# A decoder step on one core: the opening of the kernel, where the input is turned and split

## The chip, the cores and the metric

The kernel runs on one core of one Trainium2 chip. The metric is the time of one execution in microseconds (us) of device time; several executions are made and the median is taken. The profile of one execution gives, for each engine of the core, when each instruction ran: TensorE (PE, matrix products, with its weight loads shown apart as PEld), VectorE (DVE), ScalarE (ACT), GpSimd (POOL) and SyncE (SP, which here only issues transfers). An engine's letters with a q behind them (ACTq, SPq) are its queue, which issues transfers and waits.

## The reference

A two-layer decoder makes one step for a prompt of 512 tokens and for 8 samples of one token each, all in float32 and with the same weights. Layer 0 mixes tokens by causal pooling, layer 1 by sliding-window attention with sinks. Both layers have a SwiGLU block before and after the mixer. Only the first block matters for what follows:

```python
D_MODEL = 1024
D_FF = 2816

def _rmsnorm(x, g):
    xf = x.astype(jnp.float32)
    y = xf * lax.rsqrt(jnp.mean(xf * xf, axis=-1, keepdims=True) + EPS)
    return (y * g.astype(jnp.float32)).astype(x.dtype)

def _swiglu(x, wg, wu, wd):
    return (jax.nn.silu(x @ wg) * (x @ wu)) @ wd

x = x + 0.5 * _swiglu(_rmsnorm(x, norm_g[l, 0]), ffn_w_gate[l, 0], ffn_w_up[l, 0], ffn_w_down[l, 0])
```

## The kernel before, in words

**Layout.** Tokens lie along the free side: 512 prompt tokens and 8 samples make 520 columns, and the 1024 features make 8 tiles of 128 partitions, `x[0]` to `x[7]`. Each float32 operand of a product is split into a high part and a low part, and a product is made of three terms: high by high, low by high, high by low. ScalarE makes the high part (a copy that rounds), VectorE the low part (the rest). For the input the names are `xh` and `xl`, for a piece of 128x512 weights `wh` (line 194) and `wl` (line 195). The 520 columns are taken as two halves of 260, so one feature tile against one weight piece is six products of 260 columns (line 417).

**The opening (lines 657 to 736).** The input arrives as rows, so it must be turned. `load_x(eng, c, b2)` loads a block `xt` of two token tiles by 256 features; there are 4 columns `c` by 2 halves `b2`, and each block serves two feature tiles. `xs` are the samples' rows, `grow` the rows of the norms' gains, `grow2` three more rows of gains needed later. `W.begin(2)` issues the first two weight pieces, half of the gate and half of the up weights of the first output tile.

Then come twelve products of a tile of ones with itself (line 698), whose result nobody reads, the turn of the gains (line 699) and their copy `gT` (line 700). `x_tile(k)` turns one feature tile: four transposes (line 707) and one for the samples (line 709) into a pair of PSUM banks, `px`. Then ScalarE writes `xh` from the bank, scaled by the gain (line 712), the bank is copied to `x[k]` (odd k: ScalarE, line 714; even k: VectorE, line 716), and VectorE writes `xl` from `x[k]` (line 717).

The loop over the eight tiles makes the first tile of the gate and up outputs together, two accumulators called `first`. In round k it makes the six products of the gate output, turns tile k+2, and makes the six products of the up output. Its first weight pieces are fetched with `W.get()`, which splits a piece into `wh` and `wl`, ahead of the loop.

**What sets the order.** A scheduler orders each engine's instructions by a model of their times; everything wrapped in `later(...)` keeps its place in the program's order on its engine. Engines run their own list strictly in order and wait on semaphores. Transfers are issued by the SP, ACT and POOL lists in their order; every eighth transfer of SP and ACT together waits for the landing of the one eight before it. PSUM has four pairs of banks (`duo()`): one goes to the ones and the gains, two to `first`, the others turn over between feature tiles. A pair is free again once all its readers are done. In the built programs, before and after the change, the accumulator of the up output lies in the pair that tile 0 was turned in.

**What follows the loop.** The squares of each `x[k]` are summed for the norm (line 366 on ScalarE, lines 368 and 370 on VectorE), the next output tile runs `plain_tile`, and so on through the blocks.

Of the kernel before, what the change touches and what calls it, by code (L numbers as in the profile page):

```python
# [11 lines left out]
F32 = mybir.dt.float32  # L12
# [3 lines left out]
ALU = mybir.AluOpType  # L16
AX = mybir.AxisListType

P = 128
D = 1024  # L20
KT = 8
# [191 lines left out]
def yoco_step(ctx, tc, ins, outs):  # L213
    nc = tc.nc
# [3 lines left out]
    V, S, T = nc.vector, nc.scalar, nc.tensor  # L218
# [8 lines left out]
    def duo():  # L227

        cnt[0] += 1
        return psp.tile([P, 2, 512], F32, tag="ps", name=f"ps{cnt[0]}")  # L230
# [4 lines left out]
    def pair(tags, shape, dtype=F32R):  # L235

        return tuple(big.tile(shape, dtype, tag=t, name=t) for t in tags)
# [13 lines left out]
    def later(ins):  # L251

        return tc.keep_in_program_order(ins)
# [52 lines left out]
    for t in range(0, 8, 2):  # L306
        gp, i = t // 4, t % 4
# [39 lines left out]
    x = [cp.tile([P, TOK], F32, name=f"x{k}") for k in range(KT)]  # L347
    gT = cp.tile([P, 72], F32, name="gT")

    def gcol(n, k):  # L350
        return gT[:, n * 8 + k : n * 8 + k + 1]
# [12 lines left out]
    def square(k, pool, tag, order=lambda ins: ins):  # L364
        sq = pool.tile([P, TOK], F32, tag=tag, name="sq", bufs=1 if tag == "rp0" else 2)
        S.activation(sq, x[k], AF.Square)
        if k == 0:
            order(V.tensor_copy(acc[:, :TOK], sq))
        else:
            order(V.tensor_tensor(acc[:, :TOK], acc[:, :TOK], sq, op=ALU.add))  # L370
# [42 lines left out]
    def mm(w, kk, mov, banks, first, last, halves=(0, 1), pin=lambda ins: ins):  # L413

        for i, (a, b) in enumerate(terms(w, mov)):
            for hf in halves:
                ins = T.matmul(  # L417
                    banks[:, hf, :H],
                    a[:, kk, :],
                    hcols(b, hf),  # L420
                    start=(first and i == 0),
                    stop=(last and i == 2),
                )
                pin(ins)
# [202 lines left out]
    def ff_pool():  # L627
        return tc.tile_pool(name="ff", bufs=2)
# [31 lines left out]
    with ff_pool() as tmp:  # L660

        xv = x_prompt[0].rearrange("(b p) c -> p b c", p=P)
        xt = {}

        def load_x(eng, c, b2):
            xt[c, b2] = big.tile([P, 2, 256], F32, tag=TT[b2], name="xt")
            later(eng.dma_start(xt[c, b2], xv[:, 2 * b2 : 2 * b2 + 2, c * 256 : (c + 1) * 256]))

        grow = tmp.tile([48, P], F32, tag="g", name="grow")
        grow2 = tmp.tile([24, P], F32, tag="g", name="grow2")  # L670
        later(nc.scalar.dma_start(grow, norm_g.rearrange("l n (k p) -> (l n k) p", p=P)))
        xs = [big.tile([NS, 512], F32, tag=t, name="xs") for t in HH]
        for i in range(2):
            later(nc.scalar.dma_start(xs[i], x_sample[:, 0, i * 512 : (i + 1) * 512]))
        for b2 in range(2):
            load_x(nc.sync, 0, b2)
        W.begin(2)
        warm = cp.tile([P, 1], F32, name="warm")
        later(S.activation(warm, ones[:, 0:1], AF.Square))
        for b2 in range(2):  # L680
            load_x(nc.scalar, 1, b2)
        for b2 in range(2):
            load_x(nc.sync, 2, b2)
        W.load(0)
        for b2 in range(2):
            load_x(nc.sync, 3, b2)
        W.load(2)
        nc.gpsimd.dma_start(grow2[0:8, :], kv_norm_g.rearrange("(k p) -> k p", p=P))
        nc.gpsimd.dma_start(grow2[8:16, :], final_norm_g.rearrange("(k p) -> k p", p=P))
        nc.gpsimd.dma_start(grow2[16:24, :], pool_scale.rearrange("l (k p) -> (l k) p", p=P))  # L690
        sinks = cp.tile([P, 64], F32, name="sinks")
        nsinks = cp.tile([P, 64], F32, name="nsinks")
        sink_s = cp.tile([P, 2], F32, name="sink_s")
        sraw = cp.tile([P, 16], F32, name="sraw")
        mov0, tt = [], {}
        pd = duo()
        for i in range(12):
            later(T.matmul(pd[:, 1, :P], ones, ones, start=True, stop=True))  # L698
        later(T.transpose(pd[:, 0, :48], grow, ident[:48, :48]))
        later(S.copy(gT[:, :48], pd[:, 0, :48]))  # L700

        def x_tile(k):

            pd = duo()
            for b in range(NB):
                src = xt[k // 2, b // 2][:, b % 2, (k % 2) * P : (k % 2 + 1) * P]
                later(T.transpose(pd[:, 0, b * P : (b + 1) * P], src, ident))
            src = xs[k // 4][:, (k % 4) * P : (k % 4 + 1) * P]
            later(T.transpose(pd[:, 1, :NS], src, ident[:NS, :NS]))
            px = pd.rearrange("p b c -> p (b c)")[:, :TOK]  # L710
            xh, xl = pair(XX, [P, TOK])
            later(S.activation(xh, px, AF.Copy, scale=gcol(0, k)))
            if k % 2:
                later(S.copy(x[k], px))
            else:
                later(V.tensor_copy(x[k], px))
            later(V.scalar_tensor_tensor(xl, x[k], gcol(0, k), xh.bitcast(F32), op0=ALU.mult, op1=ALU.subtract))  # L717
            mov0.append((xh, xl))

        W.pin = later  # L720
        first = duo(), duo()
        x_tile(0)
        ws = [W.get()]
        x_tile(1)
        ws.append(W.get())
        for k in range(KT):
            if k == 3:
                ws = [ws[0], ws[1], W.get(), W.get()]
            for o, banks in enumerate(first):
                mm(ws[k // 4 * 2 + o], k % 4, mov0[k], banks, k == 0, k == KT - 1, pin=later)  # L730
                if not o and k + 2 < KT:
                    x_tile(k + 2)
            if k > 4:
                W.prefetch()
        W.pin = lambda ins: ins
        for k in range(KT):
            square(k, tmp, "g")
        pd = duo()
        T.transpose(pd[:, 0, 48:72], grow2, ident[:24, :24])
        S.copy(gT[:, 48:], pd[:, 0, 48:72])  # L740

        prep = {}
        sel = cp.tile([P, 34], F32, name="sel")
        sts = cp.tile([P, KT, NS], F32, name="sts")

        def pool_prep():

            wp3 = pool_w[0].rearrange("g (k p) c -> p (g k) c", p=P)

            def raw(shape, src):  # L750
                r = splp.tile(shape, F32, tag="S", name="pr", bufs=4)
                nc.scalar.dma_start(r, src)
                return r

            st = [raw([120, 512], state_pool[0, :, :, i * 512 : (i + 1) * 512].rearrange("b r c -> (b r) c")) for i in (0, 1)]
            nc.scalar.dma_start(sel, consts[:, C_SEL : C_SEL + 34])
            pst = ps()
            for k in range(KT):
                T.matmul(
                    pst[:, k * NS : (k + 1) * NS],  # L760
                    st[k // 4][:, (k % 4) * P : (k % 4 + 1) * P],
                    sel[:120, (k // 2) * NS : (k // 2 + 1) * NS],
                    start=True,
                    stop=True,
                )
            V.tensor_copy(sts, pst[:, : KT * NS].rearrange("p (k s) -> p k s", k=KT))
            yield
            raws = []
            for i in range(4):
                raws.append(raw([P, 2, 256], wp3[:, 2 * i : 2 * i + 2, :]))  # L770
            for i in range(4):
                prep["w", i] = pair(TT, [P, 2, 256])
                split(prep["w", i], raws[i])
                raws.append(raw([P, 512], bands[:, i, :512]))
                yield
            for i in range(4):
                G = big.tile([P, B_T], F32R, tag="th", name="G")
                S.activation(G[:, :512], raws[4 + i], AF.Copy)
                prep["G", i] = G
                raws.append(raw([P, B_W - 512], bands[:, i, 512:]))  # L780
            yield
            for i in range(4):
                S.activation(prep["G", i][:, 512:], raws[8 + i][:, : B_T - 512], AF.Copy)
                bt = big.tile([P, 2, 256], F32R, tag="tl", name="bt")
                split((bt[:, 0, :], bt[:, 1, :]), raws[8 + i][:, B_T - 512 :])
                prep["T", i] = bt
                if i % 2:
                    yield

        after = deferred(1, tmp, "g", XX, mov1, TW)  # L790
        ffn(0, tmp, mov0, start_hooks(tmp, 0, tt, 2), tt, HH, after, pool_prep(), first)
# [661 lines left out]
```

## Time and profile before

| | us |
|---|---|
| median of 3 executions | 1692.24 |
| lowest and highest | 1691.66 and 1692.97 |
| profiled execution, its own time | 1691.85 |
| its span, first to last instruction | 1690.0 |
| PE busy in the span | 1657.5 |
| DVE busy | 1254.4 |
| ACT busy | 903.5 |

The span is the time on the core between the first and the last instruction; 1.85 us lie around it. A line of the timeline gives the start, the time taken, the engine, the line of the kernel, the operation, what it writes and reads, how often, and in brackets how long the engine had been idle and who ended that. A line of the stretches gives the window, its length, each engine's busy time with the number of instructions, and the granted share of TensorE's clock. A busy PE is one with an instruction in it; the ends of products are modelled.

### The profile page before, as it was taken

What the parts mean: (1) busy time and instruction counts of PE and PEld (TensorE: products, weight loads), DVE (VectorE), ACT (ScalarE), POOL (GpSimd) and SP (SyncE); (2) the same over time, 40 slices, a digit from 0 to 9 for tenths busy, and PEclk for the clock granted to TensorE, in tenths of its full rate; (3) what the DMA queues carried; (4) which work ended last, traced back from release to release, by engine and by line L of the source; (5) the groups of instructions that cost most, each with busy time, mean ns of one, the idle gap of its engine ahead of it and who ended that gap; (6) DMA issues with size and microseconds to landing.
All of it is one profiled execution on the core that took longest, in us unless ns stands there. A gap on an engine that the chain in (4) does not pass through costs nothing.

```text
span 1690.0 us, 34449 instructions
## 1 busy us (share of the span) xinstructions
PE 1657.5 (98%) x13754; PEld 1642.7 (97%) x13754; DVE 1254.4 (74%) x2452; ACT 903.5 (53%) x1793; POOL 142.3 (8%) x176
## 2 busy tenths in 40 slices
PE   9999999999999999999999999999989999999997
PEld 8999999999999999999999999998879999999996
DVE  6866866887875875888775875888876885785776
ACT  6743643665652652656552652655886653463454
POOL 0101101000101101100101101100000100110100
PEclk9999999999999999999999999999899999999998
DMA  8546745652545855634745845642122554674631
GB/s 214 137 128 142 181 134 136 174 167 80 129 140 129 178 147 130 153 117 129 162 137 125 187 137 127 152 138 71 50 51 76 131 137 131 148 173 132 148 109 52
DMA packets 313327, 224.71 MB, mean 133 GB/s; under 512 B 9152, under 2 KB 289320, under 8 KB 313126
## 3 DMA queue, kind: packets, MB, share of 16 engines
q1 hardware_dynamic: 286416, 176.13, 36.8%
q0 software_dynamic: 22432, 40.26, 14.5%
q10 hardware_dynamic: 4318, 6.12, 1.2%
q8 instruction: 108, 1.77, 0.4%
q14 instruction: 53, 0.43, 0.1%
HBM read 180.11 MB, written 5.04 MB: 110 GB/s over the span
## 4 chain that ended last, share of the span: by engine, by line
PE 90%; DVE 4%; ACT 3%; DMA 1%; issue 1%; DVEq 0%; ACTq 0%
PE ps L443 45%; PE ps L417 41%; ACT sm L1121 1%; PE ps L1169 1%; PE ps L814 1%; DVE wl L195 1%; DMA pr<-in_bands_dram 1%; PE ps L839 1%; DVE sm L1101 1%; DVE xl L246 0%; ACT wh L194 0%; PE ps L1146 0%; PE ps L381 0%; PE ps L698 0%; DMA pr<-in_pool_w_dram 0%
## 5 line engine op out<-in xcount | busy, mean ns | idle before, releaser
L194 ACT ACTIVATE wh<-raw 128x512 fp32r<-128x512 f32 (+1 forms) x736 | 446.3, 621 | 544.8 <-PE ps L417 329.5
L195 DVE TENSOR_TENSOR wl<-raw,wh 128x512 fp32r<-128x512 f32 (+1 forms) x736 | 486.9, 676 | 200.7 <-ACT wh L194 197.2
L443 PE MATMUL ps<-th,wh 128*128 128x260 f32 x1216 | 343.7, 283 | 0.0
L443 PE MATMUL ps<-tl,wh 128*128 128x260 f32 x1216 | 343.1, 282 | 0.0
L443 PE MATMUL ps<-th,wl 128*128 128x260 f32 x1216 | 341.5, 282 | 0.0
L417 PE MATMUL ps<-hh,wh 128*128 128x260 f32 x1376 | 284.3, 285 | 2.3 <-DVE mx L1101 1.0
L417 PE MATMUL ps<-hl,wh 128*128 128x260 f32 x1376 | 283.2, 283 | 0.0
L417 PE MATMUL ps<-hh,wl 128*128 128x260 f32 x1376 | 280.7, 282 | 0.0
L443 PEld LDWEIGHTS ps<-tl,wh 128*128 128x128 f32 x1216 | 229.0, 188 | 0.0
L443 PEld LDWEIGHTS ps<-th,wh 128*128 128x128 f32 x1216 | 228.7, 188 | 0.2 <-ACT sa L523 0.2
L443 PEld LDWEIGHTS ps<-th,wl 128*128 128x128 f32 x1216 | 228.1, 188 | 0.0
L417 PEld LDWEIGHTS ps<-hh,wh 128*128 128x128 f32 x1376 | 213.5, 189 | 4.0 <-DVE mx L1101 1.2
L417 PEld LDWEIGHTS ps<-hl,wh 128*128 128x128 f32 x1376 | 215.2, 189 | 0.1
L417 PEld LDWEIGHTS ps<-hh,wl 128*128 128x128 f32 x1376 | 214.0, 189 | 0.0
L443 PE MATMUL ps<-xh,wh 128*128 128x260 f32 x672 | 188.3, 283 | 0.0
L443 PE MATMUL ps<-xl,wh 128*128 128x260 f32 x672 | 188.2, 283 | 0.0
L443 PE MATMUL ps<-xh,wl 128*128 128x260 f32 x672 | 184.2, 282 | 0.0
L159 POOL DMA_DIRECT2D raw<-raw x76 | 65.5, 862 | 1302.8 <-DMA raw<-in_ffn_w_up_dram 438.9
L417 PE MATMUL ps<-xh,wh 128*128 128x260 f32 x736 | 149.4, 285 | 0.6 <-ACT wh L194 0.6
L417 PE MATMUL ps<-xl,wh 128*128 128x260 f32 x736 | 149.5, 284 | 0.5 <-DVE xl L717 0.5
L417 PE MATMUL ps<-xh,wl 128*128 128x260 f32 x736 | 147.8, 283 | 0.1
L591 DVE TENSOR_TENSOR u<-ps,R 128x520 f32<-128x520 f32 (+1 forms) x99 | 67.2, 681 | 106.3 <-PE ps L417 106.3
(260 smaller groups left out, 2849.1 us busy)
## 6 DMA issues: line engine op xcount, KB each, us to landing
raw<-in_ffn_w_gate_dram SPq DMA_DIRECT2D x87, 512.0 KB, 3.9
raw<-in_ffn_w_up_dram SPq DMA_DIRECT2D x87, 512.0 KB, 5.4
raw<-in_ffn_w_down_dram SPq DMA_DIRECT2D x32, 1024.0 KB, 5.3
raw<-raw POOLq DMA_DIRECT2D x76, 256.0 KB, 3.3
S<-in_ffn_w_up_dram SPq DMA_DIRECT2D x76, 256.0 KB, 5.6
S<-raw POOLq DMA_DIRECT2D x76, 256.0 KB, 4.7
raw<-in_ffn_w_down_dram SPq DMA_DIRECT2D x16, 768.0 KB, 4.9
raw<-in_w_q_dram SPq DMA_DIRECT2D x8, 512.0 KB, 4.0
```

The lines of the kernel that those rows point to most:

```text
L159: G.dma_start(blk(raw, 2, 1), blk(raw, 1, 1), accum_op=ALU.add)
L194: self.pin(nc.scalar.activation(dh, src, AF.Copy))
L195: self.pin(nc.vector.tensor_tensor(dl, src, dh.bitcast(F32), op=ALU.subtract))
L417: ins = T.matmul(banks[:, hf, :H], a[:, kk, :], hcols(b, hf), start=(first and i == 0), stop=(last and i == 2),)
L443: T.matmul(bank[:, :H], a[:, kk, :], b, start=(not more and kk == 0 and i == 0), stop=(kk == 3 and i == 2), skip_group_check=more,)
L591: V.tensor_tensor(parts(u), bank[:, hfs[0] : hfs[-1] + 1, :H], parts(R[:, c]), op=ALU.mult)
L814: T.matmul(o, a[:, s], b[:, kk, :], start=(n == 0), stop=(n == 5))
L839: T.matmul(po[:, half * 256 : half * 256 + 256], z[:, tau, c], b, start=(i == 0), stop=(i == len(lst) - 1),)
L1101: ins = V.tensor_tensor_reduce(out=sm[:, e * 256 : (e + 1) * 256], in0=self.pe[e][:, bi * 256 : (bi + 1) * 256], in1=cst[:, mk : mk + 256] ...
L1121: S.activation(part(i), part(i), AF.Exp, scale=r8[:, b : b + 1], bias=nm[:, i : i + 1], accum_out=den[:, i : i + 1],)
L1169: T.matmul(po[:, bi * 256 : (bi + 1) * 256], a, p_[:, kc_], start=(n == 0), stop=(n == 3 * len(kts) - 1),)
```

## The change

Four edits, all in the opening:

1. Seven products of ones in place of twelve.
2. `xl` is written from the PSUM bank and no longer from `x[k]`. The copy to `x[k]` is put off: `x_tile` returns it as a function, and round k of the loop calls it after the gate output's six products, just ahead of turning tile k+2.
3. The two loads of `x`'s second column on ACT's list stand ahead of the small activation `warm` that brings ScalarE's table in; they stood behind it.
4. The three loads of `grow2` on POOL's list keep the program's order, behind the making of the identity matrix.

```diff
         W.begin(2)
+        for b2 in range(2):
+            load_x(nc.scalar, 1, b2)
         warm = cp.tile([P, 1], F32, name="warm")
         later(S.activation(warm, ones[:, 0:1], AF.Square))
-        for b2 in range(2):
-            load_x(nc.scalar, 1, b2)
...
-        nc.gpsimd.dma_start(grow2[0:8, :], kv_norm_g.rearrange("(k p) -> k p", p=P))
+        later(nc.gpsimd.dma_start(grow2[0:8, :], kv_norm_g.rearrange("(k p) -> k p", p=P)))
...
-        for i in range(12):
+        for i in range(7):
             later(T.matmul(pd[:, 1, :P], ones, ones, start=True, stop=True))
...
             later(S.activation(xh, px, AF.Copy, scale=gcol(0, k)))
-            if k % 2:
-                later(S.copy(x[k], px))
-            else:
-                later(V.tensor_copy(x[k], px))
-            later(V.scalar_tensor_tensor(xl, x[k], gcol(0, k), xh.bitcast(F32), op0=ALU.mult, op1=ALU.subtract))
+            later(V.scalar_tensor_tensor(xl, px, gcol(0, k), xh.bitcast(F32), op0=ALU.mult, op1=ALU.subtract))
             mov0.append((xh, xl))
+
+            def copy():
+                if k % 2:
+                    later(S.copy(x[k], px))
+                else:
+                    later(V.tensor_copy(x[k], px))
+
+            return copy
...
-        x_tile(0)
+        copies = [x_tile(0)]
         ws = [W.get()]
-        x_tile(1)
+        copies.append(x_tile(1))
         ws.append(W.get())
         for k in range(KT):
...
                 mm(ws[k // 4 * 2 + o], k % 4, mov0[k], banks, k == 0, k == KT - 1, pin=later)
-                if not o and k + 2 < KT:
-                    x_tile(k + 2)
+                if not o:
+                    copies.pop(0)()
+                    if k + 2 < KT:
+                        copies.append(x_tile(k + 2))
```

In the built program the lists of all engines change in two places alone: in the opening, and for some 24 us of the attention stage, where the scheduler puts the softmax of the samples and of the prompt's blocks in another order.

More of the change, by code (lines that the diff above doesn't have):

```diff
@@ L687, in yoco_step @@
         W.load(2)
-        nc.gpsimd.dma_start(grow2[0:8, :], kv_norm_g.rearrange("(k p) -> k p", p=P))
-        nc.gpsimd.dma_start(grow2[8:16, :], final_norm_g.rearrange("(k p) -> k p", p=P))
-        nc.gpsimd.dma_start(grow2[16:24, :], pool_scale.rearrange("l (k p) -> (l k) p", p=P))
+        later(nc.gpsimd.dma_start(grow2[0:8, :], kv_norm_g.rearrange("(k p) -> k p", p=P)))
+        later(nc.gpsimd.dma_start(grow2[8:16, :], final_norm_g.rearrange("(k p) -> k p", p=P)))
+        later(nc.gpsimd.dma_start(grow2[16:24, :], pool_scale.rearrange("l (k p) -> (l k) p", p=P)))
         sinks = cp.tile([P, 64], F32, name="sinks")
```

## The prediction

> **What bounds the kernel now.** I read the page first (shares and chain), then the opening's timeline engine by engine, then the waits, then TensorE's clock by stretches.
>
> ```profile
> PE 1657.5 (98%) x13754; PEld 1642.7 (97%) x13754; DVE 1254.4 (74%) x2452; ACT 903.5 (53%) x1793; POOL 142.3 (8%) x176
> ...
> PE 90%; DVE 4%; ACT 3%; DMA 1%; issue 1%; DVEq 0%; ACTq 0%
> ```
>
> TensorE is the bound: 98% busy and 90% of the chain that ended last. A delay of TensorE in the opening is paid in full, since its later work is a row of products with few waits. So the question is when TensorE does each feature tile in the opening:
>
> ```profile
> 1.06 4.72 PE L698 MATMUL ps<-ones 128*128 128x128 f32 x24 [1.06 <-DVE acc L346]
> ...
> 4.04 0.40 ACTq L667 DMA_DIRECT2D xt<-in_x_prompt_dram  x1
> ...
> 7.40 0.62 ACT L194 ACTIVATE wh<-raw 128x512 fp32r<-128x512 f32 x1
> ...
> 8.07 0.50 PE L417 MATMUL ps<-xh,wh 128*128 128x260 f32 x2 [0.63 <-ACT wh L194]
> ...
> 9.09 0.51 PE L417 MATMUL ps<-xl,wh 128*128 128x260 f32 x2 [0.51 <-DVE xl L717]
> ...
> 9.61 0.63 ACT L194 ACTIVATE wh<-raw 128x512 fp32r<-128x512 f32 x1 [0.52 <-DMA raw<-in_ffn_w_up_dram]
> ...
> 10.04 0.60 PE L707 MATMUL ps<-ident,xt 128*128 128x128 f32 x4
> ...
> 10.28 0.69 DVE L195 TENSOR_TENSOR wl<-raw,wh 128x512 fp32r<-128x512 f32 x1
> ...
> 10.72 0.51 PE L417 MATMUL ps<-xh,wh 128*128 128x260 f32 x2
> ...
> 12.27 0.60 PE L707 MATMUL ps<-ident,xt 128*128 128x128 f32 x4
> ...
> 14.63 0.60 PE L707 MATMUL ps<-ident,xt 128*128 128x128 f32 x4
> ...
> 16.85 0.60 PE L707 MATMUL ps<-ident,xt 128*128 128x128 f32 x4
> ```
>
> The first product waits for `wh`, and that for the gate weights, which land just before 7.40; the up weights land just before 9.61. These two landings, not the ones, set the start. From 9.69 on TensorE has no wait: the turns (L707) come every 2.2 to 2.4 us, at 10.04, 12.27, 14.63, 16.85, 19.07 and 21.31 for tiles 2 to 7. In each period TensorE has 12 products 0.12 apart (1.44) and a turn (0.7).
>
> The clock has a rule of its own here:
>
> ```profile
> 4.81:8.22 3.41, 2.78 (x21) 1.00 0.99 314
> ...
> 376.86:380.27 3.41, 1.77 (x15) 1.00 0.86 312
> 380.27:383.69 3.42, 3.42 (x19) 0.50 0.59 190
> ...
> 1182.41:1185.82 3.41, 2.94 (x18) 0.50 0.84 211
> 1185.82:1189.23 3.41, 1.85 (x7) 0.50 0.50 96
> ...
> 1233.61:1237.02 3.41, 1.56 (x13) 1.00 0.46 135
> 1237.02:1240.43 3.41, 3.05 (x14) 0.50 0.88 175
> ```
>
> In windows of 3.41 us the granted clock falls to 0.50 after one with TensorE busy 1.77 or 1.56 us; it stays full after 2.30 us (373.45 to 376.86). From half it came back after 3.05 and 3.42 us and not after 2.94 or 1.85. It also starts at half: the records of ones start 0.21 us apart up to 4.8 and 0.11 after.
>
> **The change part by part.** *Five products of ones fewer* take 10 records away. At the first 0.213 us each, the 14 left end at 1.43 + 13 x 0.213 = 4.2, and TensorE can turn tile 0 when its second block lands (the second SP load is known to be in at 5.08, when SP issues the load that waits for it). Tiles 0 and 1 are turned by 6.3 and not 7.4. Gain on the path: nothing, since the first product waits for the gate weights (7.40). The cover is that landing. What is lost is activity: between 6.3 and 8.07 TensorE is idle.
>
> *The loads ahead of the table load.* ACT's list issued them at 2.25 and 4.04 although the table load started at 2.18: the queue runs ahead of the engine. The second load still waits for the first block of x, so it is issued at 4.04 again; value 0. Bounds: the first one 0.07 earlier, and up to 0.4 later or earlier landings from how the transfers share the engines. The table load (1.28) with `warm` (0.20) and `gT` (0.20) moves to 4.45 to 6.15; `xh` of tile 0 can run at 6.2 to 6.9 (6.81 before), hidden under the wait for 7.40. *The loads of grow2 on POOL* start some 0.3 us later (behind a 0.31 us operation that then runs earlier); they are needed at 23 us: 0.
>
> *xl from the bank.* The same instruction with another source: 0.76 (L717). A like one that reads a bank (L502, 128x520) takes 0.70, so 0.70 to 0.76; I take 0.76. For tile 0 the copy of 0.70 leaves the path: `xl` 6.9 to 7.7, `wl` 8.05 to 8.74, so the six gate products end at 9.1 and tile 2 is turned from 9.14 (its second block is only in by 9.56) to 10.1. This is the gain, 0.9 us at this point.
>
> *The copy put off.* Here it is lost. The up accumulator lies in tile 0's pair of banks. Before, the copy of tile 0 was done at 8.25; now it stands on VectorE's list behind the second `wl`. That one waits for the up weights: `wh` 9.61 to 10.24, `wl` 10.28 to 10.97, then the copy at 10.89 + 0.70 = 11.59 (VectorE starts the next about 0.61 after a 0.69 one). The first up product, 10.72 before, is at 11.64: **+0.9**.
>
> From then on each turn of tile k+2 waits for the copy of tile k, which stands behind `xl` of tile k+1 on VectorE or behind it and weights on ScalarE. Steps: a turn's start to `xh` 0.79 (12.27 to 13.05), `xh` 0.69, `xl` 0.76 with the next 0.67 after its start, copy 0.70 (VectorE) or 0.59 (ScalarE).
>
> - Tile 3: 11.64 + 1.54 = 13.18 (12.27 before: +0.9).
> - Tile 4: `xh` of 3 at 13.97, `xl` 14.69, copy of 2 at 15.36 to 16.06, turn 16.10 (14.63: +1.5). TensorE is ready at 15.5.
> - Tile 5: `xh` of 4 at 16.89, two `wh` behind it 0.52 apart, copy of 3 at 18.53 to 19.12, turn 19.15 (16.85: +2.3).
> - Tile 6: `xh` of 5 at 19.94, `xl` 20.66, copy of 4 to 22.03, turn 22.07 (19.07: +3.0).
> - Tile 7: squares of 4 at 22.06, a scaled copy (0.72), `xh` of 6 at 23.21, copy of 5 to 24.39, turn 24.42 (21.31: +3.1).
>
> Then the loop's products run to 28.85. The next output tile needs the up accumulator's banks: in the new list ScalarE has four `wh`, one more `wh` that waits for a product at 28.0, the copy of tile 7, another `wh`, then the copy out (L490), 29.62 to 30.20. First product of the next tile 30.25. Before, this tile had tile 7's banks and began at 24.87 among the last of the loop's. 72 products then come before the norm's sums (L381): 30.25 + 72 x 0.1205 + 0.1 = 39.0 against 34.72: **+4.3**. Bounds by the same rows: if each of the five put-off copies were hidden, +0.9; if each step took 0.1 more, +5.3.
>
> *The clock.* TensorE would be busy 5.08 to 6.35 and 8.07 to 8.22 of the window to 8.22: 1.4 of 3.41 us, less than the 1.56 and 1.77 that were followed by half clock. The next one has about 2.3 at half pace, less than the 2.94 that did not bring it back; so half clock to 15.05. The 12 products from 11.64 take 2.6 and not 1.5, and part of the turn of tile 3 doubles: **+1.5**, which the chain behind it hands on. Bounds: 0, and 2.0 when the windows lie later. [...]
>
> *The attention's new order.* The same instructions; 2.7 us of TensorE idle lie in that stretch (20.48 - 17.75 in 1243.85 to 1264.33). Bounds: -2.7, and +3.2 (one more window at half clock 1.7, and waits 1.5). I take 0, as the units' chains keep their lengths.
>
> Sum: +4.3 + 1.5 = +5.8, on the profiled execution's 1691.85: **1697.7**. That execution is 0.4 below the median.
>
> **The rivals.** [...] *The put-off copies are hidden*, so only the gain stays: it decides at 10.24, when the second `wh` is done; if tile 0's copy were done by then, the first up product were at 10.29, 0.43 earlier: 1691.4, not slower. For it: VectorE is idle 0.69 us around 11.3 before. Against: the list puts the copy behind `wl`, which cannot start before 10.28. *Attention gains its idle time*: 1691.85 + 5.8 - 2.7 = 1695.0. *Attention loses*: 1691.85 + 5.8 + 3.2 = 1700.9. *The loads do nothing* is in the forecast.
>
> **How the numbers follow.** Forecast 0.55, full clock 0.2, attention gains 0.1, attention loses 0.08, copies hidden 0.07. The range goes from the full clock with the attention's whole gain (1693.5) to the attention's loss (1700.9). 0.2% is 3.4 us, about what a measurement can tell: slower means over 1695.6. That holds in the forecast, the loss, and most of the full clock (0.75); within it are the attention's gain and the rest (0.21); faster needs the copies hidden and the attention's gain at once (0.04).
>
> **What would show it.** Right: an idle time of TensorE before the first up product put down to the copy at line 720, at about 11.6; turns of tiles 4 to 7 about 2.9, 3.0, 2.9 and 2.4 apart, each released by a copy; a wait of over 1 us before the next output tile, released by line 490; the sums of line 381 at 39 to 41; a granted clock of 0.50 between 8 and 15. Wrong: turns still 2.2 apart, or line 381 before 36. The forecast fails most easily at the clock, and in the attention, where the opening's rows say nothing.

## The result, and the profile after

The changed kernel takes 1703.66 us (median of 5, 1702.91 to 1704.93) where the kernel before takes 1692.38 (median of 5, 1691.66 to 1692.97): the medians lie 11.3 us apart, and the ratio, estimated from the executions, is 1.0058, 95% interval 1.0044 to 1.0072, or 9.8 us. The forecast was 1697.7, the range ended at 1700.9. The sign is right, the size is about half. The profiled execution took 1704.93 us, the longest of the five; its span is 1702.9, 12.9 more than the span before.

From the page of the kernel after, the busy time of the engines and the chain by engine:

```profile
PE 1665.3 (98%) x13744; PEld 1648.9 (97%) x13744; DVE 1254.3 (74%) x2452; ACT 905.5 (53%) x1793; POOL 142.6 (8%) x176
...
PE 89%; DVE 4%; ACT 4%; DMA 2%; issue 1%; DVEq 0%; ACTq 0%
```

TensorE is still the bound. It is busy 7.8 us longer with ten records fewer, and its mean granted clock is 0.989 and not 0.992, so part of the loss is time at half clock; the other 5 us are idle time.

The opening on TensorE's timeline (start, time taken, engine, line, operation; in brackets the idle time before and who ended it):

```profile
1.05 3.36 PE L698 MATMUL ps<-ones 128*128 128x128 f32 x14 [1.05 <-DVE acc L346]
...
8.01 0.80 PE L417 MATMUL ps<-xh,wh 128*128 128x260 f32 x2 [0.65 <-ACT wh L194]
...
10.34 0.69 PE L707 MATMUL ps<-ident,xt 128*128 128x128 f32 x2 [0.23 <-DMA xt<-in_x_prompt_dram]
...
11.16 0.80 PE L417 MATMUL ps<-xh,wh 128*128 128x260 f32 x2
...
13.92 1.05 PE L707 MATMUL ps<-ident,xt 128*128 128x128 f32 x4
...
17.41 0.63 PE L707 MATMUL ps<-ident,xt 128*128 128x128 f32 x4
...
20.50 0.66 PE L707 MATMUL ps<-ident,xt 128*128 128x128 f32 x4 [0.68 <-ACT x L718]
...
23.54 0.63 PE L707 MATMUL ps<-ident,xt 128*128 128x128 f32 x4 [0.62 <-issue]
...
25.91 0.66 PE L707 MATMUL ps<-ident,xt 128*128 128x128 f32 x4
...
31.76 0.51 PE L417 MATMUL ps<-xh,wh 128*128 128x260 f32 x2 [0.78 <-ACT t L490]
...
40.55 1.17 PE L381 MATMUL ps<-ones,acc 128*128 128x1 f32 x10
```

The turns (L707) are no longer 2.2 apart but 3.5, 3.1, 3.0 and 2.4, and before those of tiles 5 and 6 TensorE waits 0.6 to 0.7. One wait is put down to the copy of an odd tile (L718). The other is marked "issue"; VectorE's timeline shows what it was, the copy of an even tile, which ends at 23.44, 0.1 ahead of the turn at 23.54:

```profile
22.75 0.69 DVE L720 COPY x<-ps 128x520 f32<-128x520 f32 x1
```

The sums of line 381 come at 40.55 and not at 34.72: +5.8, as forecast. But the delay does not stay there. If the start of each TensorE instruction is set against the start of the same instruction before (my working, from the two traces), it is 5.8 late at 35, 6.3 at 377, 7.9 at 390, 8.1 up to 1236 and **13.0 from 1275 to the end**. So 1.5 is lost near 380 and 4.9 in the attention, where the forecast had nothing. Near 380 the stretches (window, length, TensorE's busy time, granted clock, two DMA columns) are:

```profile
381.81:385.22 3.41, 0.40 (x4) 1.00 0.99 302
385.22:388.63 3.41, 3.41 (x17) 0.50 0.95 344
388.64:392.05 3.41, 3.41 (x17) 0.50 0.41 162
```

Two windows at half clock, where the kernel before had one.

In the attention, the same stretch of work in the profile before and then in the profile after:

```profile
1237.40:1280.10 42.70, 39.50 (x325) 0.96 0.27 63
```

```profile
1245.50:1293.10 47.60, 42.17 (x325) 0.89 0.25 57
```

The same 325 records take 4.9 longer: 2.7 of it busy time, as the mean clock falls from 0.96 to 0.89, and 2.2 idle time. The waits of TensorE there (what waits, for whom; sum, times, longest), before:

```profile
PE ps L1169 <- DVE mx L1101: 1.5, 1, 1.5
PE ps L417 <- DVE mx L1101: 1.0, 1, 1.0
PE ps L1232 <- DVE sT L1222: 0.7, 1, 0.7
...
PE ps L417 <- ACT pr L1237: 0.3, 1, 0.3
```

and after (line numbers are 6 higher):

```profile
PE ps L1175 <- DVE oS L1271: 1.8, 1, 1.8
PE ps L1175 <- DVE mx L1107: 1.5, 1, 1.5
PE ps L1238 <- DVE sT L1228: 1.3, 1, 1.3
PE ps L1152 <- ACT pr L1243: 1.3, 1, 1.3
```

The chain of waits says how the softmax of the samples (`pr`) got late. Before, it runs behind one exp of a unit:

```profile
1247.14 0.69 ACT sm L1121 x2
1247.86 0.47 ACT pr L1237 x2
```

After, ScalarE's list has all four exps of the unit first:

```profile
1254.34 2.45 ACT sm L1127 x8
1256.79 0.34 ACT pr L1243 x2
```

The longest wait, 1.8 for `oS` (the copy that frees the bank of the samples' values), comes of a second swap, on VectorE's list. Before, the copy stands ahead of `den`, the sum that needs a unit's four exps:

```profile
1260.38 0.53 DVE L1265 COPY oS<-ps 64x16 f32<-64x16 f32 x4 [1.23 <-PE ps L1254]
1261.57 0.17 DVE L1130 TENSOR_TENSOR den<-den,es 128x4 f32<-128x4 f32 x1 [0.66 <-ACT es L1129]
```

After, it stands behind it, and so waits for the exps too:

```profile
1271.57 0.16 DVE L1136 TENSOR_TENSOR den<-den,es 128x4 f32<-128x4 f32 x1 [2.41 <-ACT es L1135]
1271.65 0.52 DVE L1271 COPY oS<-ps 64x16 f32<-64x16 f32 x4
```

In the two traces the lists differ from 1244.1 (VectorE) to 1282.8 (TensorE) by the times of before, which is 39 us and not some 24.

So there are three places to explain: the opening, the windows near 380, and the attention's new order.

### The profile page after: what moved, and what is told of

Same layout as the page of the kernel before. It is cut to its first block, busy times and chain, and to the rows that moved or that the text cites. A ratio compares the mean times of both kernels' runs of the same rounds, so it can differ in the third digit from the quotient of the medians.

```text
span 1702.9 us, 34428 instructions
## 1 busy us (share of the span) xinstructions
PE 1665.3 (98%) x13744; PEld 1648.9 (97%) x13744; DVE 1254.3 (74%) x2452; ACT 905.5 (53%) x1793; POOL 142.6 (8%) x176
## 4 chain that ended last, share of the span: by engine, by line
PE 89%; DVE 4%; ACT 4%; DMA 2%; issue 1%; DVEq 0%; ACTq 0%
PE ps L443 45%; PE ps L417 40%; ACT sm L1127 2%; PE ps L820 1%; DMA pr<-in_bands_dram 1%; DVE wl L195 1%; PE ps L845 1%; PE ps L1175 1%; DVE sm L1107 1%; DVE xl L246 1%; DMA xt<-in_x_prompt_dram 1%; ACT wh L194 0%; PE ps L381 0%; PE ps L1152 0%; DVE u L591 0%
```

## The experiments

Two theories stood against each other. **T**: about half of the loss is made in the opening, the other half by the new order in the attention. **R**: all of it follows from the opening; a later start shifts everything against the clock's windows, and the order costs nothing.

In this table "late" is the start of the same TensorE instruction against the first profile of before, in us, from one profile of each kernel (my working); "stretch" is the time of the same attention work (1237.4 to 1280.1 before), with the time at half clock in it. The time is the median, with before's median of the same chip behind it; the ratio with its interval is estimated from the executions and is not the quotient of the two medians; e1 to e4, e5 to e8 and e9 to e12 each share a chip.

| run | late at L381 | at 390 | at 1236 | at 1275 | stretch | at half clock | us, before's us | ratio |
|---|---|---|---|---|---|---|---|---|
| before (first profile) | 0 | 0 | 0 | 0 | 42.7 | 3.1 | | |
| after (first profile) | 5.8 | 7.9 | 8.1 | 13.0 | 47.6 | 10.1 | 1703.7, 1692.4 | 1.0058 (1.0044 to 1.0072) |
| e1_pin_before | -0.4 | -0.1 | -0.4 | 4.0 | 47.1 | 9.8 | 1697.0, 1694.9 | 1.0020 (1.0008 to 1.0032) |
| e2_pin_after | 5.5 | 7.2 | 7.2 | 11.5 | 47.0 | 9.7 | 1702.7, 1694.9 | 1.0048 (1.0033 to 1.0062) |
| e3_before_bank | 0.4 | 0.6 | 0.4 | 5.4 | 47.7 | 10.0 | 1697.7, 1694.9 | 1.0020 (1.0010 to 1.0030) |
| e4_after_ones12 | 5.5 | 7.1 | 6.5 | 11.5 | 47.8 | 9.9 | 1701.4, 1694.9 | 1.0044 (1.0029 to 1.0060) |
| e5_before_again | 2.0 | 2.4 | 1.6 | 1.6 | 42.7 | 3.3 | 1693.5, 1694.5 | 0.9996 (0.9984 to 1.0007) |
| e6_no_put_off | 1.9 | 2.4 | 2.6 | 7.6 | 47.8 | 9.8 | 1699.3, 1694.5 | 1.0025 (1.0015 to 1.0035) |
| e7_after_warm | 4.7 | 3.7 | 2.6 | 8.6 | 48.8 | 12.4 | 1700.7, 1694.5 | 1.0035 (1.0023 to 1.0047) |
| e8_after_fill | 4.8 | 7.6 | 7.8 | 9.5 | 44.5 | 6.7 | 1701.7, 1694.5 | 1.0038 (1.0024 to 1.0052) |
| e9_after_again | 4.9 | 5.3 | 5.1 | 11.7 | 49.3 | 16.4 | 1704.2, 1693.6 | 1.0064 (1.0051 to 1.0076) |
| e10_after_order | 4.9 | 5.1 | 5.3 | 5.2 | 42.7 | 3.0 | 1698.3, 1693.6 | 1.0029 (1.0017 to 1.0041) |
| e11_before_warm | 0.3 | 0.7 | 0.7 | 0.7 | 42.7 | 3.2 | 1694.6, 1693.6 | 1.0002 (0.9993 to 1.0011) |
| e12_best | 1.2 | 1.2 | 1.0 | 4.0 | 45.7 | 12.9 | 1695.1, 1693.6 | 1.0011 (1.0000 to 1.0022) |

Single executions of before lay between 1690.9 and 1698.7 on these chips, so a profile is one draw from some 8 us, and the last two columns are the ones that tell a kernel from another.

### The attention's order

**e1_pin_before, e2_pin_after.** The scheduler's order hangs on its model of all that came earlier. Two statements for VectorE are kept in the program's order, in the kernel before and in the changed one; then all lists outside the opening are the same in both:

```diff
-            V.tensor_tensor(
+            ins = V.tensor_tensor(
                 sT4[:, g, b0 : b0 + 4, :],
...
+            if g and b0:
+                later(ins)
...
-            split(tuple(a[:, :SP] for a in z), oT[t])
+            S.activation(z[0][:, :SP], oT[t], AF.Copy)
+            later(V.tensor_tensor(z[1][:, :SP], oT[t], z[0][:, :SP].bitcast(F32), op=ALU.subtract))
```

> The kernel before, with two instructions of the attention on VectorE kept in the program's order, so that the attention's order can be held the same with either opening. Both theories: the opening as before, the sums of line 381 at 34.7. Theory T (of the +11.3 about 6 come from the opening and about 5 from the attention's new order): the pinned order is a third one, and its price shows between 1243 and 1275 alone; 1690 to 1697. Theory R (all of it follows from the opening, the order costs nothing): 1692.4, within 1.

> The changed kernel with the same two instructions kept in order; outside the opening all engines' lists are those of the run above. T: the run above + 6.0 (sums of line 381 at 40.5, 5.8 later), or + 7.6 if the longer half clock near 380 comes again. R: the run above + 11.

The two differ by 5.7 in the median and not by 11, so the opening alone does not make the loss. The pinned order has its own price with the old opening too: 47.1 for the stretch in place of 42.7.

**e3_before_bank.** One line of the change in the kernel before, by which the scheduler comes to the changed kernel's attention order:

```diff
-            later(V.scalar_tensor_tensor(xl, x[k], gcol(0, k), xh.bitcast(F32), op0=ALU.mult, op1=ALU.subtract))
+            later(V.scalar_tensor_tensor(xl, px, gcol(0, k), xh.bitcast(F32), op0=ALU.mult, op1=ALU.subtract))
```

> The kernel before with one edit: xl is read from the bank, the copy stays ahead of it. Its attention has the changed kernel's order. In the opening the first up product comes some 0.4 earlier (10.3). T: 1692.4 - 0.4 + 4.9 = 1696.9, with the loss between 1243 and 1275. R: 1692.0, and no loss there.

The opening is all but unchanged, and the stretch takes 47.7 with 10 us at half clock: late by 0.4 at 1236, by 5.4 at 1275. The first up product came at 11.31, not at 10.3. The time is 1.0020 times before's.

**e9_after_again, e10_after_order.** The kernel after once more, and with one more product of ones ahead of the sums of a later norm. That shifts the scheduler's model just so that the attention gets the kernel before's own order, on all engines (the lists also differ from 773 to 799, where the added product stands; the delay is 5.1 at 390 and 5.3 at 1236):

```diff
-                rstd_tok()
+                rstd_tok(fill=1)
...
+        for i in range(fill):
+            T.matmul(pss_[0][:, 1, :P], ones, ones, start=True, stop=True)
```

> The changed kernel itself, beside the kernel before on one chip, for its own spread and a second profile. If the first profile was typical: sums of line 381 at 40.2 to 40.6, a second window at half clock near 384, a loss of 4.9 between 1243 and 1275, times 1702.9 to 1704.9.

> The changed kernel with one more product of ones ahead of the sums of a later norm (0.2 us; nobody reads it). With it the scheduler comes to the kernel before's own order in the whole attention, on all engines; the opening stays the changed one. T (the new order costs 4.9 in itself): no loss between 1243 and 1275, the changed kernel less 4.7, that is 1699.0. Rival S (the first profile of before had a lucky clock in the attention, and the order costs 2 to 3, as the medians of the two earlier orders above before say): the changed kernel less 2 to 3. R (the order costs nothing): the changed kernel, within 1.

e9's time lies where it was expected. Its profile does not fit as well: line 381 came at 39.61 and not at 40.2 or later, no second window at half clock came near 384 (late by 4.9 at line 381 and by 5.3 at 390), and the stretch took 6.6 more than before's and not 4.9.

The changed opening with the old order (e10) loses nothing in the attention: late by 5.3 at 1236 and by 5.2 at 1275. Its stretch:

```profile
1242.60:1285.30 42.70, 39.45 (x326) 0.96 0.28 63
```

That is before's stretch again, in length and in clock. The time falls from 1704.2 to 1698.3, by 6.0, on one chip. R is out: with the late opening kept, the loss goes with the order. This pair speaks against rival S (2 to 3); e3 against before, 1.0020 or 3.4 with 1.7 to 5.1, lies between it and T. So the order costs 3.4 to 6.0 by the times, and 4.9 to 6.6 in the two profiles of the kernel after.

### The opening

**e4_after_ones12, e7_after_warm, e6_no_put_off.** These part the half clock from the put-off copies. e4 has twelve ones again. e7 also fills the gap ahead of the first product. e6 keeps seven ones and puts the copies straight behind `xl`:

```diff
-        for i in range(7):
+        for i in range(12):
             later(T.matmul(pd[:, 1, :P], ones, ones, start=True, stop=True))
```

```diff
         copies.append(x_tile(1))
+        for i in range(5):
+            later(T.matmul(first[0][:, 0, 384:], ones, ones, start=True, stop=True))
```

```diff
-            return copy
+            copy()
+            return lambda: None
```

> The changed kernel with twelve products of ones again; the attention has the changed kernel's order but for details. T: the clock is full from 4.8 on, the waits for the put-off copies stay: sums of line 381 at 34.7 + 4.3 = 39.0, time 1692.4 + 4.3 + 4.9 = 1701.6. If the waits come only of the half clock: sums at 34.3 to 36, time 1692.4 + 1 + 4.9 = 1698.3. R: 1692.4 + 11.3 x 4.3 / 5.8 = 1700.8.

> The changed kernel with twelve ones, and five more products of ones between the turn of tile 1 and the first product, where TensorE is idle for 1.1 us; their result is read by nobody. T: the clock stays full through the opening, the waits for the put-off copies stay, sums of line 381 at 34.7 + 4.3 = 39.0, and turns of tiles 4 to 7 released by copies. H: sums at 35 to 36.

> The changed kernel with the copies straight behind xl again (seven ones, xl from the bank, loads ahead). The attention has the changed kernel's order. T (the put-off copies are the larger part of the opening's loss): the sums of line 381 at 34.7 + 0.4 + 1.7 to 2.2 of half clock = 36.8 to 37.3, turns 2.2 to 2.4 apart from the first full-clock window on, the next output tile without a wait. Rival H (half clock in the opening makes the waits, the copies' place costs nothing): sums at 40 to 40.5, as in the changed kernel.

e7 is the clean one: no window at half clock in the opening from 6.43 on (granted 1.00 in the windows to 16.67, pairs of products of 260 columns take 0.39 to 0.51), and still

```profile
11.69 0.48 PE L417 MATMUL ps<-xh,wh 128*128 128x260 f32 x2 [0.35 <-DVE x L720]
...
16.34 0.63 PE L707 MATMUL ps<-ident,xt 128*128 128x128 f32 x4 [0.77 <-issue]
...
19.43 0.66 PE L707 MATMUL ps<-ident,xt 128*128 128x128 f32 x4 [0.67 <-ACT x L718]
...
22.48 0.63 PE L707 MATMUL ps<-ident,xt 128*128 128x128 f32 x4 [0.60 <-issue]
...
30.70 0.51 PE L417 MATMUL ps<-xh,wh 128*128 128x260 f32 x2 [0.78 <-ACT t L490]
39.45 1.17 PE L381 MATMUL ps<-ones,acc 128*128 128x1 f32 x10
```

The up product waits for the copy of tile 0 (L720), turns are 3.1 apart, and line 381 stands at 39.45, 4.7 later than in before's first profile, all at full clock. e6 is the counterpart. Its clock is half for two windows:

```profile
3.92:7.34 3.42, 2.21 (x14) 1.00 0.84 258
7.34:10.75 3.41, 2.10 (x9) 0.50 1.08 323
10.75:14.16 3.41, 3.41 (x16) 0.50 0.95 268
14.16:17.58 3.42, 3.42 (x27) 1.00 1.12 300
```

and as soon as it is full the turns are 2.2 apart, with no wait:

```profile
14.15 0.61 PE L707 MATMUL ps<-ident,xt 128*128 128x128 f32 x4
...
16.39 0.60 PE L707 MATMUL ps<-ident,xt 128*128 128x128 f32 x4
...
18.62 0.60 PE L707 MATMUL ps<-ident,xt 128*128 128x128 f32 x4
```

Line 381 comes at 36.60, 1.9 late; in five profiles with seven ones and put-off copies (after twice, e2, e8, e10) it is 4.8 to 5.8 late. These numbers hold more than the two causes, since the first up product does not start at the same time in every run. Counted from there (my working, one profile each; e12 is described below, and its opening has the copies straight behind `xl` and a full clock):

| run | copies | first up product | from there to line 381 | of that at half clock |
|---|---|---|---|---|
| before | ahead of `xl` | 10.72 | 24.0 | 0 |
| e12_best | straight behind `xl` | 11.68 | 24.3 | 0 |
| e6_no_put_off | straight behind `xl` | 11.38 | 25.2 | 2.8 |
| e7_after_warm | put off | 11.69 | 27.8 | 0 |
| e10_after_order | put off | 10.84 | 28.8 | 2.5 |
| e4_after_ones12 | put off | 11.07 | 29.2 | 3.4 |
| after | put off | 11.16 | 29.4 | 5.4 |

From the first up product on, the put-off copies cost 3.5 (e7 against e12) to 3.8 (against before) at full clock. Ahead of it they cost e7 another 0.35, the wait shown above; the other 0.6 by which e7's up product starts later than before's are not put down to a copy. Half clock costs 1.2 without put-off copies (e6) and 1.0 with them (e10) for about the same time at half clock, so these two add up. For 3.4 and 5.4 us of it the price is 1.4 and 1.6: in a longer stretch the waits take up a part, as the 0.77 ahead of tile 4's turn in e7 is gone in after. Rival H is out. e4, with twelve ones, still had one window at half clock from 11.26, after one with TensorE busy 2.23 of 3.42 us, and line 381 at 40.23.

### Near 380, and the kernel before

**e8_after_fill.** Eleven products of ones ahead of the sums at 378 (the same `fill` as in e10, at another norm).

> The changed kernel with eleven products of ones ahead of the sums of the norm at 378 (their result is read by nobody), where TensorE is idle 2.75 us. If the loss of 1.5 near 380 is a second window at half clock: no half clock there, 390 lies 4.2 to 4.6 later than before where the changed kernel lay 7.9 later. If it is something else: still 7 or more. The attention gets one more order, whose price is open; T says that it shows between 1243 and 1275 alone.

It does not answer the question: the delay at 390 is 7.6, but the gap is another one. The list puts the eleven products ahead of the last products before the gap and the sums behind those, and then TensorE waits for another engine instead:

```profile
390.74 0.39 PE L822 MATMUL ps<-th,xh 128*128 128x256 f32 x1 [3.05 <-DVE zl L249]
```

A stretch at half clock followed the new gap too: single products take 0.41 from 391.87 to 394.64, and 0.28 before and behind. What the other runs say of 380: with a late opening the second window came in after, e2 and e4, and not in e9 or e10, whose lists there are those of after; e7 had none at all. From line 381 to 390 the delay grows by 2.1, 1.7 and 1.6 in the first three, and by 0.4 and 0.2 in e9 and e10. So the 1.5 near 380 came with a second window in single executions, and not with a list; why the window came is not shown. None of the seven profiles without put-off copies had a second window (their delay grows by 0.5 at most there), so it is not ruled out that a late opening makes one likelier. (The attention's order of e8, one more, cost 1.8 in its profile.)

**e5_before_again.** The kernel before, for a second profile.

> The kernel before itself, for a second profile of it: single executions of it lay between 1691.4 and 1698.7, and the first profile is one of the short ones. If the spread is made by stretches at half clock: the profile shows the opening at 34.7 within 0.5, the lists' order unchanged, and about one more stretch of 3.41 us at half clock for every 1.7 us above 1690.0 of span. If it is made by the landings of transfers: longer waits put down to DMA and the same number of half-clock stretches.

The span was 1691.5 and the opening 2.0 late, with one window at half clock from 10.06 that the first profile did not have; elsewhere 0.4 was won back (late by 2.4 at 390 and by 1.6 at 1236), with one window at half clock fewer between 1184 and 1194. Neither expectation holds: the opening was not within 0.5 of 34.7, and the number of windows is that of the first profile (mean granted clock 0.992 in both). So the kernel before, too, had a half-clock window in its opening in one of two profiles, and was 2.0 late there. Of the 8 us between its executions this names one part; the long ones were not profiled.

**e11_before_warm.** Three more products of ones ahead of the first product, in the kernel before.

> The kernel before with three more products of ones between the turn of tile 1 and the first product, where TensorE is idle; nobody reads them. All other lists are as before. If the half clock in the opening comes of that idle time: no half clock between 5 and 20, sums of line 381 at 34.3 to 35.1; since one of two profiles of before had such a window (sums 2.0 later), the median is 0.5 to 1.5 below before. If not: the median within 0.5 of before.

The clock was full in this profile's opening (pairs of products take 0.40 to 0.51 from 8.50 on), but the time is 1.0002 times before's (0.9993 to 1.0011): nothing gained that can be measured, where 0.5 to 1.5 were expected.

**e12_best.** The parts of the change that were taken to cost nothing, with fillers and with before's order in the stretch:

```diff
+            copy()
+            return lambda: None
...
+        for i in range(4):
+            later(T.matmul(first[0][:, 0, 384:], ones, ones, start=True, stop=True))
...
-                po = ps()
+                pv = duo()
+                po = pv[:, 0, :]
+                for i in range({0: 10, 1: 0}.get(2 * self.t + self.h, 0)):
+                    T.matmul(pv[:, 1, :P], ones, ones, start=True, stop=True)
```

> Of the change: xl from the bank and the loads ahead; the copies straight behind xl, twelve ones, four more in the gap ahead of the first product, and ten ahead of the first values product of the attention, where TensorE waits 2.5 us (1179.5 to 1182). The attention's later order is the kernel before's own. T: opening at 34.3 to 35.1, one or two windows at half clock fewer at 1182 to 1192 (-1.7 to -3.4), no loss from 1243 to 1275: 2 to 4 below before. Rival: the ten products come late and delay what stands behind them, within 1 of before or above.

It is not faster than before. Its opening is 1.2 late (line 381 at 35.93) although the clock is full from 5.44 on: on ScalarE's list the second `wh` stands behind the squares, a scaled copy and the copy of tile 1, runs at 10.99, and the first up product waits for it:

```profile
11.68 0.50 PE L417 MATMUL ps<-xh,wh 128*128 128x260 f32 x2 [0.72 <-ACT wh L194]
```

Two windows at half clock fewer came between 1182 and 1193, as expected (the first profile of before has three, from 1182.41 to 1192.65), but the ten products had to wait for their bank, so they ran late:

```profile
1183.27 4.00 PE L1170 MATMUL ps<-ones 128*128 128x128 f32 x20 [2.39 <-DVE mx L1110]
```

And it shows a limit of the account above: with before's order and less idle time (2.2), the stretch took 45.7, with three more windows in it at half clock (12.9 us and not 3.1). So the order sets the waits, and the windows come on top; they are not a fixed price of an order, and what puts a window at half clock is not shown.

## Why the prediction was right and wrong

- **TensorE bound, a delay in the opening paid in full: right.** e10 carries its 4.9 of line 381 to the end as 5.2, and the time is 1.0029 times before's, 4.9 us. Single executions differ: e7's 4.7 were 3.7 at 390, with no window at half clock near 380, and 2.6 at 1236.
- **The put-off copies, forecast +4.3: right in mechanism, and near in size.** The forecast was worked out for a full clock, and e7 is that kernel. Turns of tiles 3 to 7 were forecast at 13.18, 16.10, 19.15, 22.07 and 24.42; e7 has 13.19, 16.34, 19.43, 22.48 and 24.85. The next output tile was forecast at 30.25 and starts at 30.70, after a wait of 0.78 and not of over 1; line 381 at 39.0 and stands at 39.45. The path from a turn over `xh`, `xl` and copy to the next-but-one turn is what carries it. That e7 starts it at the forecast's time is luck. From the first up product to line 381 the forecast had 3.4 more than before, and e7 has 3.8; ahead of it the forecast gave 0.9 to a copy, and e7 shows 0.35.
- **The first up product at 11.64, waiting for the copy of tile 0: right in mechanism, by chance of landings in size.** In e7 it waits 0.35, in e4 0.43, in e10 0.19. e7's 11.69 is so near the forecast because its gate weights were split at 8.17 and not at 7.40. In the profile of after it starts at 11.16 without that wait: the up weights were in earlier (`wh` at 8.85 and not at 9.61), and the copy was done at 10.81.
- **`xl` from the bank, a gain of 0.9 at tile 2: wrong.** The first six products do end earlier, but then TensorE waits for the second block of `x`'s second column (0.23 in after, 0.24 in e3, 0.28 in e7, put down to DMA). The forecast took that block to be in by 9.56; it came at 9.8 to 10.8. e3, with this edit alone, gained nothing: line 381 at 35.07 against 34.72 and 36.69 in before's two profiles.
- **The loads ahead of the table load, 0: borne out as far as it was tried.** The second load was still held back behind the first block; the pair was issued by 4.60, before by 4.44. The table load stood at 4.63 (forecast 4.45), hidden. No run has this edit, or that of `grow2`, alone.
- **The half clock, forecast +1.5 from 8.22 to 15.05: right in kind, and in size where the half clock lasted as long as forecast.** In e2 the clock was half from 8.43 to 15.26. In the profile of after the full clock did not come with the seven ones at all: the first record of it is at 16.59 (12.99 in its second profile), and the pairs of products ahead of that take 0.61 to 0.80, those behind it 0.39 to 0.51. Counted from the first up product it cost 1.4 in e4, with 3.4 us at half clock as in the forecast, and 0.6 to 1.6 in the other profiles with put-off copies. The full clock, given 0.2, did not hold in any of the six profiles with seven ones, nor in e4 with twelve: e2 was at half clock from 8.43 after a gap of 1.29, e4 from 11.26 after gaps of 1.11, 0.22 and 0.43.
- **The attention's new order, taken at 0 with bounds -2.7 and +3.2: wrong, and this is the step that failed.** It cost 4.9 in the first profile, 6.6 in the second, 6.0 by e9 against e10. The reason given, that the units' chains keep their lengths, does not hold: on ScalarE's list four exps (2.45) came to stand ahead of the samples' softmax, and on VectorE's list the copy `oS` came to stand behind a sum that needs four exps. With these lists TensorE waits 1.3 for `pr` and 1.8 for `oS`, and windows at half clock came along, one behind the wait for `oS` (from 1272.69, behind a window busy for 1.58) and one behind a window that was busy for 2.80 of 3.41 us (from 1262.45). The upper bound, one such window and 1.5 of waits, was too small on the clock's side: there were two more windows in the first profile (10.1 us at half clock against 3.1) and four in the second. Why they came is open: e12 has before's order and three more of them. The rival "attention loses", given 0.08, was what happened, and more strongly.
- **The sum.** By ratios, opening 4.9 (e10) and order 3.4 to 6.0 make 8.3 to 10.9; measured are 9.8 (7.4 to 12.2) in the first comparison and 10.8 (8.6 to 12.9) in e9. Nothing larger is left over there. e7 does not fit as well: its time is 5.9 above before's (3.9 to 8.0), less than its late opening and the order together.

## What to carry to other kernels

An edit moves more than the place it stands in when a scheduler orders the lists by modelled times: compare the built lists to the end, and give each hunk far away a price from both sides, its clock included; here one line of the opening is enough to reorder the attention (e3), and that costs about as much as all that the change does to the opening. Before putting work off, follow what the put-off instruction holds: a copy that frees a bank is on the path of whoever needs the bank next, however free its own engine is (here 3.5 to 3.8 us, e7 against e12 and before). To part two causes of lateness on one path, take one run without each, and count from the same instruction: a start that came later by itself looks like a cost.

## What the runs showed of the hardware that was not expected

- The records of half clock that end within the spans of the two first profiles last 3.41, 6.83 or 10.24 us, and they lie differently in each execution: in six profiles with the same seven ones at the start, the first record of full clock stands at 3.92, 5.02, 5.97, 6.56, 12.99 and 16.59. Near 380 no window, one or two at half clock followed in different executions: from 377 to 384 the delay falls by 1.5 in e7, which had none, and rises by 1.3 in after, which had two where before had one.
- Windows with TensorE busy 2.1 to 2.3 us were followed by half clock in the openings (2.12 in e2, 2.21 in e6, 2.27 in e5), where the forecast had read 2.30 as safe, and 1.62 in e6 (375.98 to 379.39) was followed by a full one. In the attention one busy for 2.80 us was followed by half clock in after (1259.04 to 1262.45), and one busy for 3.03 in e12 (1251.31 to 1254.72). Busy time of records alone does not tell which.
- Two orders of the same instructions differ by some 5 us in a stretch of 43, and four profiles of one of them agree to 0.1 (42.67 to 42.74) with two different openings ahead of it, while a fifth (e12) needs 45.7, 12.9 of it at half clock.
